# Turns of gates, latents, rotary keys, memory queries and conv operands by 32x32 VectorE blocks parked in DRAM, in a two-layer hybrid encoder

## The chip, the cores and the metric

The kernel runs on one core of one Trainium2 chip. Five engines matter here: TensorE (PE, with its weight loads shown apart as PEld), VectorE (DVE), ScalarE (ACT), GpSimd (POOL) and SyncE (SP). The metric is the time of one launch on the device in microseconds (us). Three runs of the kernel before took 1466.64, 1466.75 and 1467.07 us; the median is 1466.75 us.

## What is computed

Two layers of a sandwich-normalised mixer over 512 tokens of width 2048, all in fp32. Each layer projects the normalised input once into ten parts, feeds three groups of heads, gates their outputs and projects back:

```python
for l in range(DEPTH):                                     # DEPTH = 2
    h = rmsnorm(x, pre_norm_g[l])
    z = h @ w_in[l]                                        # 2048 x 4928
    q_lat, kv_lat, k_pe, gb, gc, xin, q_mem, gate = split_cols(z)
    q = (rmsnorm(q_lat, q_norm_g[l]) @ w_uq[l])            # 8 heads, rotary part turned
    kv = (rmsnorm(kv_lat, kv_norm_g[l]) @ w_ukv[l])
    a_out = mla_attention(q, k, v)                         # 8 heads, width 1024
    c_out = short_gated_conv(gb, gc, xin, conv_w[l])       # width 512
    m_out = memory_attention(q_mem, mem_n, ...)            # 4 heads, width 512
    mix = concatenate([a_out, c_out, m_out]) * silu(gate)
    x = x + rmsnorm(mix @ w_o[l], post_norm_g[l])
```

The convolution is `gb * conv3(gc * xin)`, three taps along the tokens for each channel. The latents, the rotary keys, the memory queries, the convolution and the gated mix are all needed with channels on the partitions, while the input projection leaves tokens on the partitions. So each of them has to be turned (transposed) once.

## The kernel before

**Arithmetic.** Each fp32 operand is split into a rounded part (hi) and the rest (lo), and a product is three matmuls, hi\*hi, hi\*lo and lo\*hi (`mm3`, L265 to L274). For the weights the split is made on the chip: ACT casts a piece of 128x1024 (`wh`, L189), then DVE subtracts (`wl`, L190). Each of `wh` and `wl` has three buffers; the raw pieces (`wr`) have eight, and are loaded by SP (L146), or added onto a piece that is there by a GpSimd DMA that accumulates (`more`, also L146). Where two pieces are added on the chip, DVE does so ahead of the cast (L178, the `sums` of a piece).

**The input projection** runs as five groups for each layer. A group computes a 2x2 block of column halves by seven products (a Strassen form) of combinations of the input (`P1` to `P7`). A plain group (`STEADY`) has 28 steps: four of P1, eight of P5 and P2 in turns, eight of P6 and P3 in turns, four of P7 and four of P4. Each step takes one weight piece through twelve matmuls 512 wide (416 wide in the latents' group). The order of the groups in `gs` before: 0 is gc and xi (convolution), 1 is gb and a gate, 2 is a gate `gm` with the memory queries `qm`, 3 is the latents with the rotary keys (`lat`), and 4 is the two gates `ga0` and `ga1`.

**The turns before.** gc\*xi and gb (`conv_turn`), the latents (`latent_turn`), the memory queries (`qm_turn`) are turned by PE, through `turn4` (L911 to L915): four matmuls with the identity fill one bank `tps` of 128x512, and ACT or DVE copy it out. The rotary keys go the same way (`k_rope_turn`, L1021, bank `krps`). The gates gm, ga0 and ga1 are turned already in 32x32 blocks by DVE (L933), and `exchange` (L941) then moves the blocks between partitions by sixteen DMAs from one SBUF tile to another.

**What sets the order.** Python code puts the steps one behind another. PE, SP and POOL keep that order. The instructions of DVE and ACT are put in order by a scheduler, engine by engine; at run time each engine takes its own list strictly in order. The preparation of a weight piece runs two steps ahead, its load up to eight. Small jobs that may come later are put off (`pr.defer`) and paid out beside the steps. The convolution's four chunks of 128 channels are woven into group 2, one in each second step.

The programs' names: `gc`, `gb`, `gm`, `qm`, `ga` are slabs of 128x2048, `y` is the gated mix, `P` is a PSUM bank of the projection, `ptp` a bank for turned attention probabilities, `sc` for scores, `u` and `cols` the convolution's input chunk and its taps.

## Time and profile before

The profiled execution took 1469.51 us; its span, from the first instruction to the last, is 1467.7 us.

| what | value |
|---|---|
| profiled execution / its span | 1469.51 us / 1467.7 us |
| PE busy | 1452.2 us in 7104 matmuls |
| PE weight loads | 1237.3 us |
| DVE busy | 1095.8 us in 1461 instructions |
| ACT busy | 869.6 us in 1328 instructions |
| POOL busy | 267.8 us |
| DMA | 295.22 MB, 201 GB/s on average |

A row of groups reads: line, engine, operation, output<-inputs, tile shape, number; then busy time in us and mean ns of one; then idle time ahead of them and what ended it. A matmul's duration is longer than the distance to the next one, since they are pipelined; a chain of waits shows the distance. A row of a timeline reads: start in us, duration in us, engine, line, operation, in square brackets the idle time ahead of it and what ended that. A row of the waits reads: who waited, for whom, us in total, times, longest.

### The profile page before, as it was taken

The numbers are of one execution on the slowest core, as the hardware profiler recorded it, in microseconds if no ns is written. First come the engines' busy times: TensorE is split into PE (matmuls) and PEld (weight loads), VectorE is DVE, ScalarE is ACT, GpSimd is POOL, SyncE is SP. The second block draws the span as 40 slices with busy tenths as digits, with TensorE's granted clock in tenths as the row PEclk, the third lists the DMA queues.
The fourth block names the chain that finished last, engine by engine and source line by source line (L and its number), as shares of the span: only waits on it lengthen the run. The fifth ranks groups of instructions, "written<-read, shape, count | busy, mean of one in ns | idle before, by whom it ended". The sixth has DMA issues, their size and how long they took to land.

```text
span 1467.7 us, 19472 instructions
## 1 busy us (share of the span) xinstructions
PE 1452.2 (99%) x7104; PEld 1237.3 (84%) x7104; DVE 1095.8 (75%) x1461; ACT 869.6 (59%) x1328; POOL 267.8 (18%) x272
## 2 busy tenths in 40 slices
PE   9999999999999999999999999999999999999997
PEld 7887888899888888888898888888998888888886
DVE  5899677857677778868789656766576776788687
ACT  7856445445458788654777434454464586786443
POOL 0032302031301010321220333030313001003111
PEclk9999999999999999999999999999999999999999
DMA  9999979797977292795987999696979674128983
GB/s 355 402 271 210 226 190 187 172 185 212 231 232 166 78 275 88 124 229 155 342 291 222 239 225 220 195 178 158 201 202 237 212 186 104 40 87 151 270 168 129
DMA packets 156672, 295.22 MB, mean 201 GB/s; under 512 B 11616, under 2 KB 46944, under 8 KB 152736
## 3 DMA queue, kind: packets, MB, share of 16 engines
q0 software_dynamic: 56000, 125.32, 42.7%
q1 hardware_dynamic: 100576, 168.65, 36.4%
q8 instruction: 56, 0.92, 0.3%
q14 instruction: 40, 0.33, 0.1%
HBM read 266.01 MB, written 21.63 MB: 196 GB/s over the span
## 4 chain that ended last, share of the span: by engine, by line
PE 84%; issue 5%; DMA 5%; POOL 3%; ACT 2%; DVE 1%; SPq 0%; POOLq 0%; DVEq 0%; ACTq 0%
PE P L273 20%; PE P L272 20%; PE P L274 20%; POOL wr L146 3%; DMA wr<-in_w_in_dram 3%; PE ptp L1198 2%; PE o L273 1%; PE o L274 1%; PE o L272 1%; PE sc L272 1%; PE sc L274 1%; PE sc L273 1%; PE tps L915 1%; PE sc L1179 1%; PE qps L272 1%
## 5 line engine op out<-in xcount | busy, mean ns | idle before, releaser
L190 DVE TENSOR_TENSOR wl<-wr,wh 128x1024 fp32r<-128x1024 f32 (+2 forms) x436 | 515.2, 1186 | 259.2 <-ACT wh L189 255.9
L189 ACT CAST wh<-wr 128x1024 fp32r<-128x1024 f32 (+2 forms) x436 | 443.9, 1023 | 444.5 <-PE P L274 329.4
L272 PE MATMUL P<-wh,S 128*128 128x512 f32 (+1 forms) x896 | 345.2, 385 | 0.0
L273 PE MATMUL P<-wl,S 128*128 128x512 f32 (+1 forms) x896 | 344.1, 384 | 0.8 <-DVE wl L190 0.8
L274 PE MATMUL P<-wh,S 128*128 128x512 f32 (+1 forms) x896 | 343.2, 383 | 0.0
L272 PE MATMUL P<-wh,A 128*128 128x512 f32 (+1 forms) x656 | 253.0, 386 | 0.0
L273 PE MATMUL P<-wl,A 128*128 128x512 f32 (+1 forms) x656 | 251.8, 384 | 1.2 <-DVE wl L190 1.2
L274 PE MATMUL P<-wh,A 128*128 128x512 f32 (+1 forms) x656 | 251.5, 383 | 0.0
L146 POOL DMA_DIRECT2D wr<-in_w_in_dram x132 | 158.9, 1204 | 446.1 <-DVE wl L190 272.6
L273 PEld LDWEIGHTS P<-wl,S 128*128 128x128 f32 x896 | 168.2, 188 | 31.2 <-DVE wl L190 1.8
L274 PEld LDWEIGHTS P<-wh,S 128*128 128x128 f32 x896 | 168.2, 188 | 30.2
L272 PEld LDWEIGHTS P<-wh,S 128*128 128x128 f32 x896 | 168.1, 188 | 29.9 <-ACT wh L189 0.2
L273 PEld LDWEIGHTS P<-wl,A 128*128 128x128 f32 x656 | 123.2, 188 | 23.4 <-DVE wl L190 2.0
L274 PEld LDWEIGHTS P<-wh,A 128*128 128x128 f32 x656 | 123.1, 188 | 22.3
L272 PEld LDWEIGHTS P<-wh,A 128*128 128x128 f32 x656 | 123.1, 188 | 21.8 <-ACT og L586 0.2
L146 POOL DMA_DIRECT2D wr<-in_w_o_dram x40 | 48.5, 1261 | 299.0 <-DVE wl L190 293.6
L1185 ACT ACTIVATE P<-sc,nm 128x512 f32<-128x512 f32 (+1 forms) x96 | 59.8, 623 | 28.6 <-DVE nm L1182 28.3
L1182 DVE TENSOR_REDUCE nm<-sc 128x1 f32<-128x512 f32 (+1 forms) x96 | 56.7, 594 | 14.3 <-PE sc L1180 9.0
L1188 ACT ACTIVATE P<-P,rec 128x512 f32<-128x512 f32 (+1 forms) x96 | 61.8, 660 | 8.0 <-DVE rec L1187 8.0
L1198 PE MATMUL ptp<-identr,P 128*128 128x128 f32 x320 | 46.2, 273 | 2.3 <-ACT P L1188 2.3
L1198 PEld LDWEIGHTS ptp<-identr,P 128*128 128x128 f32 x320 | 37.9, 140 | 8.9 <-ACT P L1188 3.0
L178 DVE TENSOR_TENSOR wr<-wr,wr 128x1024 f32<-128x1024 f32 (+1 forms) x36 | 42.2, 1174 | 2.6 <-DMA wr<-in_w_in_dram 2.1
(317 smaller groups left out, 2069.0 us busy)
## 6 DMA issues: line engine op xcount, KB each, us to landing
wr<-in_w_in_dram SPq DMA_DIRECT2D x128, 512.0 KB, 5.6
wr<-in_w_in_dram POOLq DMA_DIRECT2D x108, 512.0 KB, 7.5
wr<-in_w_o_dram SPq DMA_DIRECT2D x48, 512.0 KB, 6.3
wr<-in_w_o_dram POOLq DMA_DIRECT2D x40, 512.0 KB, 7.3
wr<-in_w_in_dram SPq DMA_DIRECT2D x32, 416.0 KB, 3.5
wr<-in_w_in_dram POOLq DMA_DIRECT2D x24, 416.0 KB, 6.0
wr<-in_w_mk_dram SPq DMA_DIRECT2D x15, 512.0 KB, 9.1
wr<-in_w_mv_dram SPq DMA_DIRECT2D x15, 512.0 KB, 10.5
```

The lines of the kernel that those rows point to most:

```text
L146: engine.dma_start(dst, src, **kw)
L178: nc.vector.tensor_tensor(tiles[a], tiles[a], tiles[b], op=ALU.add)
L189: pin(nc.scalar.copy(hi[:, h], src[:, h]))
L190: pin(nc.vector.tensor_tensor(lo[:, h], src[:, h], hi[:, h].bitcast(F32), op=ALU.subtract))
L272: nc.tensor.matmul(ps, ah, bh, start=first, stop=False, **kw)
L273: nc.tensor.matmul(ps, ah, bl, start=False, stop=False, **kw)
L274: nc.tensor.matmul(ps, al, bh, start=False, stop=last, **kw)
L915: nc.tensor.transpose(ps[:, t * P:(t + 1) * P], v[:, 4 * j:4 * j + 4].rearrange("p g j -> p (g j)") if len(v.shape) == 3 else v[:, j * P:( ...
L1182: nc.vector.tensor_reduce(nmax, ps, axis=AX.X, op=ALU.max, negate=True)
L1185: nc.scalar.activation(pt, ps, AF.Exp, bias=nmax, accum_out=tot)
L1188: nc.scalar.activation(pt, pt, AF.Copy, scale=rec)
L1198: nc.tensor.transpose(ps[:, k * P:(k + 1) * P], pt[:, k * P:(k + 1) * P], G["ident"])
```

## The change

The latents, the rotary keys, the memory queries and the convolution's two operands are no longer turned on PE. Each such slab, and each gate, is turned by DVE in 32x32 blocks (`STREAM_TRANSPOSE`), then one DMA parks it in DRAM (`sent`), and four DMAs fetch it back, a block row each (`fetched`). The columns of `w_in` and two norm gains are permuted on the host, so that the blocks fall where they are needed. What is fetched has its tokens in a permuted order; the matmuls read it through a view of four runs of 128 (`spots`). The convolution's chunks, the memory queries and the latents are computed from fetched slabs. The latents' group becomes the third of a layer and the group gm/qm the fourth. The weight block B22 of a `STEADY` group is loaded by SP once, with P6, and a sum on DVE adds it to T, where before SP loaded it for P3 and a GpSimd DMA accumulated it for P6. The left operand of the output projection is split in two halves in layer 0 too.

```diff
@@ Left.split
             if self.apart:
-                hi, lo = (t[:, o:o + 1024].rearrange("p (t g j) -> p g t j", t=2, j=32) for o in (0, 1024))
-                split_to(hi, lo, src.rearrange("p g (t j) -> p g t j", j=32))
+                if src.shape[-1] == P:
+                    split_to(t[:, :1024], t[:, 1024:], src.rearrange("q g k -> q (g k)"))
+                    return
...
+                for i in range(2):
+                    split_to(hi[:, i], lo[:, i], src[:, :, 32 * i:32 * i + 32].rearrange("q (p c) j -> q p c j", p=4))
@@ group
+            if passes is STEADY and q in ("P6", "P3"):
+                return of("T", [("B22", "B22")], sums=[("T", "B22")]) if q == "P6" else of("B22")
             return {"P5": ..., "P6": lambda: of("T", more="B22"),
@@ input projection
+        def turned(name, t):
+            def f():
+                nc.vector.transpose(C[name][:, t], C[name][:, t])
...
-            group(L, (l, 2), 512, block((O_G + 1536, O_QM), 512), slot_of("gm", "qm"), STEADY, fin_m),
-            group(L, (l, 3), 416, block((0, 416), 416), lat, STEADY, skip),
+            group(L, (l, 2), 416, block((0, 416), 416), lat, STEADY, skip),
+            group(L, (l, 3), 512, block((O_G + 1536, O_QM), 512), slot_of("gm", "qm"), STEADY, fin_m),
@@ turns
-    def turn4(view, j, dst=None):
...
-    def exchange(dst, src):
-        for p in range(4):
-            for b in range(4):
...
-                nc.sync.dma_start(dst[32 * b:32 * b + 32, :, P * p:P * p + P], a)
+    def spots(t, c=4):
+        return t.rearrange("q (p c k) -> q c p k", p=4, c=c)
+    def sent(key, *parts):
...
+            nc.sync.dma_start(d[:, :, o:o + w].rearrange("b q k -> q b k"), t.rearrange("q (b k) -> q b k", b=4))
+    def fetched(key, name, c=4):
+        t, d = slab(name), G.pop(("sent", key))
+        for b in range(4):
+            nc.sync.dma_start(t[32 * b:32 * b + 32, :512 * c].rearrange("i (p k) -> i p k", p=4),
+                              d[b].rearrange("(p i) k -> i p k", p=4))
+        return t
-    def conv_turn(l, c, C):
-            ps = turn4(lambda t: C["gc"][:, t], c)
...
+    def conv_back():
+        G["uw"] = fetched("gc", "u")
+        G["ys"][2] = spots(fetched("gb", "y"))
+    def conv(l, c):
+            u, y, w, g = scrap("u"), scrap("conv"), G[f"cw{l}"], G["ys"][2][:, c]
+            nc.scalar.copy(by_tokens(u), spots(G["uw"])[:, c])
             nc.scalar.activation(y, u, AF.Copy, scale=w[:, 1, c:c + 1])
...
+            nc.vector.tensor_tensor(g, by_tokens(y), g, op=ALU.mult)
@@ order of a layer
-        conv = [(conv_turn(l, c, C), []) for c in range(4)]
-        put(weave(gs[2][1] + gs[2][2], conv, 2), *gs[2][3:])
+        steps = [s for passes in gs[3] for s in passes]
+        put(steps[:2])
+        add(lambda l=l, C=C: latents_begin(l, C))
...
+        add(conv_back)
+        put(steps[8:12])
+        if l == 0:
+            add(tables_turned)
+        put(steps[12:14])
+        add(conv(l, 0))
+        put(steps[14:17])
+        add(lambda l=l: latents_sent(l))
+        put(steps[17:19])
+        add(conv(l, 1))
+        put(steps[19:22])
+        add(conv(l, 2))
+        put(steps[22:25])
+        add(conv(l, 3))
+        put(steps[25:])
...
-        G["left"] = Y = Left(False, l + 1 < depth)
+        G["left"] = Y = Left(False, True)
```

**PE, group gm/qm before, layer 0.** The rows stand in the second pass of the group, where the first convolution chunk is turned. `P` are the projection's banks, `S` is a left operand, `tps` the banks of the turns.

```order
L273 MATMUL P_92_1937<-wl_1893,A_29_624 128x512
L274 MATMUL P_92_1937<-wh_1892,A_29_624 128x512
L915 MATMUL tps_1950<-identr,gc_651 128x128 x4
L915 MATMUL tps_1961<-identr,gb_867 128x128 x4
L272 MATMUL P_89_1916<-wh_1911,S_59_1007 128x512
L273 MATMUL P_89_1916<-wl_1912,S_59_1007 128x512
L274 MATMUL P_89_1916<-wh_1911,S_59_1007 128x512
```

In the changed kernel these matmuls, and the other 152 of their kind, are gone, and nothing stands in their place on PE.

**DVE before, the same place.** `wl` is the lower part of a weight piece, L956, L957 and L960 are one chunk of the convolution.

```order
L190 TENSOR_TENSOR wl_1969<-wr_1714,wh_1968 128x1024
L956 SCALAR_TENSOR_TENSOR y_1955<-u_1956,cols,y_1955 128x511
L957 SCALAR_TENSOR_TENSOR y_1955<-u_1956,cols,y_1955 128x511
L960 TENSOR_TENSOR y_1955<-y_1955,tps_1961 128x4x4x32
L190 TENSOR_TENSOR wl_1988<-wr_1852,wh_1987 128x1024
L190 TENSOR_TENSOR wl_2021<-wr_1732,wh_2020 128x1024
L956 SCALAR_TENSOR_TENSOR y_1955<-u_2008,cols,y_1955 128x511
L957 SCALAR_TENSOR_TENSOR y_1955<-u_2008,cols,y_1955 128x511
L960 TENSOR_TENSOR y_1955<-y_1955,tps_2013 128x4x4x32
L190 TENSOR_TENSOR wl_2040<-wr_1890,wh_2039 128x1024
```

One chunk stands between each second pair of weight pieces.

**DVE after, group gm/qm (now the fourth), layer 0.** `wl_2761` belongs to the sixteenth step of the group (the second of P3), `wl_2788` to the seventeenth (the third of P6); L975, L976 and L978 are the three instructions of a chunk, L178 the sum of T and B22 for the pieces of P6.

```order
L190 TENSOR_TENSOR wl_2761<-wr_2582,wh_2760 128x1024
L975 SCALAR_TENSOR_TENSOR conv_2780<-u_2779,cols,conv_2780 128x511
L976 SCALAR_TENSOR_TENSOR conv_2780<-u_2779,cols,conv_2780 128x511
L975 SCALAR_TENSOR_TENSOR conv_2880<-u_2879,cols,conv_2880 128x511
L976 SCALAR_TENSOR_TENSOR conv_2880<-u_2879,cols,conv_2880 128x511
L975 SCALAR_TENSOR_TENSOR conv_2943<-u_2942,cols,conv_2943 128x511
L976 SCALAR_TENSOR_TENSOR conv_2943<-u_2942,cols,conv_2943 128x511
L978 TENSOR_TENSOR y_2639<-conv_2780,y_2639 128x4x128
L978 TENSOR_TENSOR y_2639<-conv_2880,y_2639 128x4x128
L978 TENSOR_TENSOR y_2639<-conv_2943,y_2639 128x4x128
L178 TENSOR_TENSOR wr_2311<-wr_2311,wr_2644 128x1024
L975 SCALAR_TENSOR_TENSOR conv_3010<-u_3009,cols,conv_3010 128x511
```

Straight behind them come the second sum and the pieces that follow.

```order
L178 TENSOR_TENSOR wr_2329<-wr_2329,wr_2680 128x1024
L190 TENSOR_TENSOR wl_2788<-wr_2311,wh_2787 128x1024
L190 TENSOR_TENSOR wl_2805<-wr_2644,wh_2804 128x1024
L190 TENSOR_TENSOR wl_2823<-wr_2329,wh_2822 128x1024
L976 SCALAR_TENSOR_TENSOR conv_3010<-u_3009,cols,conv_3010 128x511
L978 TENSOR_TENSOR y_2639<-conv_3010,y_2639 128x4x128
L190 TENSOR_TENSOR wl_2845<-wr_2680,wh_2844 128x1024
```

Three whole chunks and the first instruction of the fourth now stand between two neighbouring weight pieces, with two of the new sums. In layer 1 the same rows stand between the same two steps.

**ACT after, the same place.** `wh_2760` and `wh_2787` are the upper parts of the same two pieces; L973 and L974 are ACT's two instructions of a chunk.

```order
L189 CAST wh_2760<-wr_2582 128x1024
L973 COPY u_2779<-u_2634 128x512
L974 ACTIVATE conv_2780<-u_2779,cols 128x512
L973 COPY u_2879<-u_2634 128x512
L974 ACTIVATE conv_2880<-u_2879,cols 128x512
L973 COPY u_2942<-u_2634 128x512
L974 ACTIVATE conv_2943<-u_2942,cols 128x512
L973 COPY u_3009<-u_2634 128x512
L974 ACTIVATE conv_3010<-u_3009,cols 128x512
L189 CAST wh_2787<-wr_2311 128x1024
L189 CAST wh_2804<-wr_2644 128x1024
```

All four chunks stand ahead of `wh_2787`, which is cast from the piece `wr_2311` that the sum in the DVE rows writes.

More of the change, by code (lines that the diff above doesn't have):

```diff
@@ L907, in mem_fetch, with by_tokens @@
             G[n] = t.rearrange("p (s i c) -> p s i c", s=2, i=k)
-    def turn4(view, j, dst=None):
-        ps = bank("tps")
-        for t in range(NT):
-            v = view(t)
-            nc.tensor.transpose(ps[:, t * P:(t + 1) * P], v[:, 4 * j:4 * j + 4].rearrange("p g j -> p (g j)") if len(v.shape) == 3 else v[:, j * P:(j + 1) * P], G["ident"])
-        return ps
-    def y_slab(k):
-        if k not in G["ys"]:
-            G["ys"][k] = slab("y").rearrange("p (j c) -> p j c", j=4)
-        return G["ys"][k]
+    def spots(t, c=4):
+        return t.rearrange("q (p c k) -> q c p k", p=4, c=c)
+    def by_tokens(a):
+        return a.rearrange("q (p k) -> q p k", p=4)
     def of_tiles(a):
@@ L1470, in use @@
             G["ys"] = {}
+            for n in ("cq", "ckv", "Qm"):
+                G.pop(n, None)
         ms = mem_steps(l)
@@ L1589, in encoder @@
-        put(g4[2:8])
-        add(lambda C=C: k_rope(C))
-        put(g4[8:13])
-        add(gate_rows(3, "gm", C))
-        put(g4[13:16])
-        lat = [latent_turn(l, "cq", j) for j in range(4)] + [latent_turn(l, "ckv", j) for j in range(2)] + [k_rope_turn]
-        more = [(f, []) for f in lat + [qm_turn(j, C) for j in range(4)]]
-        put(weave(g4[16:], more, 2, 2)[:-2])
+        add(latents_back)
+        put(g4[2:6])
+        add(sent_rows("qm", C))
+        put(g4[6:8])
+        add(sent_rows("gm", C))
@@ L1597, in encoder @@
+        put(g4[8:9])
+        add(latents_parts)
+        put(g4[9:14])
+        add(lambda: G.update(qmw=fetched("qm", "QmL")))
+        put(g4[14:19])
+        add(qm_parts)
+        put(g4[19:22])
+        add(gate_back(3, "gm"))
+        put(g4[22:26])
         add(mem_fetch)
-        put(weave(g4[16:], more, 2, 2)[-2:])
-        G["left"] = Y = Left(False, l + 1 < depth)
+        put(g4[26:])
+        add(lambda: pr.until(lambda: "Qm" in G and "cq" in G))
+        G["left"] = Y = Left(False, True)
```

218 lines of the change are left out of this document (120 added, 98 removed).

## The prediction

> **What bounds the kernel now.** I read the page's busy times first, then the waits, then one step of the projection in the timeline.
>
> ```profile
> PE 1452.2 (99%) x7104; PEld 1237.3 (84%) x7104; DVE 1095.8 (75%) x1461; ACT 869.6 (59%) x1328; POOL 267.8 (18%) x272
> ...
> POOL wr L146 <- DVE wl L190: 566.2, 112, 82.7
> ACT wh L189 <- PE P L274: 332.5, 235, 2.2
> ...
> PE P L273 <- DVE wl L190: 1.9, 3, 0.8
> ...
> 448.11 0.44 PE L1198 MATMUL ptp<-identr,P 128*128 128x128 f32 x2 [1.13 <-ACT P L1188]
> ```
>
> TensorE is the bound: it stands idle for 1467.7 - 1452.2 = 15.5 us of the whole span. The waits say the same from the other side. ACT's casts wait 235 times for PE to let go of a weight buffer, while PE waits for a lower part on three occasions, 1.9 us in all. The longest gap in front of a PE matmul that I found is 1.13 us. So POOL's 566.2 us of waiting costs nothing, and only two things can move the end: work that leaves or joins PE, and a new stall of PE. Stalls that exist can give back at most 15.5 us.
>
> ```profile
> 388.69 1.05 ACT L189 CAST wh<-wr 128x1024 fp32r<-128x1024 f32 x1 [1.04 <-PE P L274]
> 391.41 1.05 ACT L189 CAST wh<-wr 128x1024 fp32r<-128x1024 f32 x1 [1.67 <-PE P L274]
> ...
> 387.54 1.18 DVE L190 TENSOR_TENSOR wl<-wr,wh 128x1024 fp32r<-128x1024 f32 x1
> 388.64 0.70 DVE L933 STREAM_TRANSPOSE ga<-ga 128x512 f32<-128x512 f32 x1
> ...
> 392.50 1.23 DVE L190 TENSOR_TENSOR wl<-wr,wh 128x1024 fp32r<-128x1024 f32 x1 [1.50 <-ACT wh L189]
> ```
>
> This is the rhythm of a 512-wide step: PE frees a buffer every 391.41 - 388.69 = 2.72 us, and the lower part that is made in it is ready at 392.50 + 1.23, which is 2.32 us after PE let go. With three buffers, a piece that starts when PE leaves step n is needed by step n+3. PE has then three steps to do, 3 x 2.72 = 8.16 us, so **the slack of a weight piece is 8.16 - 2.32 = 5.84 us**. Whatever holds DVE up for less is free.
>
> **What leaves PE.**
>
> ```profile
> L915 PE MATMUL tps<-identr,lat 128*128 128x128 f32 x48 | 6.2, 272 | 0.0
> L915 PE MATMUL tps<-identr,gb 128*128 128x128 f32 x32 | 4.8, 273 | 0.0
> L915 PE MATMUL tps<-identr,gc 128*128 128x128 f32 x32 | 4.8, 271 | 0.0
> ...
> L915 PE MATMUL tps<-identr,qm 128*128 128x128 f32 x32 | 4.5, 274 | 0.0
> ...
> 225.74 0.87 PE tps L915 x8
> ...
> 421.21 0.64 PE krps L1021 x8
> ```
>
> 144 turns through `tps` and 16 through `krps` go (48+32+32+32 of the first). Their mean of 272 ns isn't the price, since matmuls overlap; the chain of waits has the distance. Eight of the first took 0.87 us, so 144 take 144 x 0.109 = 15.7 us; eight of the second took 0.64, so 16 take 1.3 us. They stand on the path, since PE is never out of work beside them: **-17.0 us**. With no new stall that is the whole effect.
>
> **What joins PE.** No matmul is added, but many read their moving operand in four runs of 128 instead of one run of 512. The nearest rows:
>
> ```profile
> L272 PE MATMUL mk<-mH,wh 128*128 128x256 f32 x128 | 36.4, 284 | 0.0
> ...
> L272 PE MATMUL vps<-wh,ckv 128*128 128x256 f32 x64 | 18.1, 282 | 0.0
> ```
>
> The values' matmul (`vps`) reads its 256 columns in two runs of 128 with a gap between, the keys' matmul of the memory (`mk`) in one piece; 282 against 284 ns. I take 0, and bound it by those 2 ns each way, times some hundreds of matmuls: under 1 us.
>
> **What joins DVE, and what covers it.**
>
> ```profile
> L933 DVE STREAM_TRANSPOSE ga<-ga 128x512 f32<-128x512 f32 x16 | 11.1, 702 | 1.3 <-ACT ga L786 1.3
> ...
> L178 DVE TENSOR_TENSOR wr<-wr,wr 128x1024 f32<-128x1024 f32 (+1 forms) x36 | 42.2, 1174 | 2.6 <-DMA wr<-in_w_in_dram 2.1
> ...
> 220.00:240.00 20.00, 20.00 (x102) 16.84 (x101) 13.27 (x14) 10.76 (x13) 3.57 (x3) 1.00 0.94 209
> 280.00:300.00 20.00, 20.00 (x100) 18.35 (x99) 18.96 (x42) 10.96 (x16) 1.18 (x1) 1.00 0.53 139
> ```
>
> Turns: 24 more of 128x512 (gc, gb and qm, four tiles in each of two layers) at 0.702 us are 16.8 us. The latents' slabs, 3584 columns for each layer, are 7 such lengths, 4.9 us, twice 9.8. The sums of T and B22: three STEADY groups of four pieces in two layers, 24 at 1.17 us, 28.2 us. Together 55 us, and DVE goes from 1096 to about 1150 us, 78%. That by itself costs nothing: in the second stretch above (the columns are PE, PEld, DVE, ACT and POOL busy, then the clock, the DMA share and GB/s) DVE is busy for 18.96 of 20 us and PE still for all 20. It costs when it comes in a lump longer than 5.84 us between two weight pieces, because DVE takes its list in order.
>
> There is such a lump. In the fourth group three whole chunks of the convolution, two sums and a first instruction of the fourth chunk stand between the lower parts of the sixteenth and seventeenth step. Before, one chunk stood between two pieces:
>
> ```profile
> 226.73 0.58 ACT L954 COPY u<-tps 128x512 f32<-128x512 f32 x1
> 227.35 0.73 ACT L955 ACTIVATE y<-u,cols 128x512 f32<-128x512 f32 x1
> ...
> 226.86 1.23 DVE L190 TENSOR_TENSOR wl<-wr,wh 128x1024 fp32r<-128x1024 f32 x1 [1.49 <-ACT wh L189]
> 228.11 0.75 DVE L956 SCALAR_TENSOR_TENSOR y<-u,cols,y 128x511 f32<-128x511 f32 x1
> 228.89 0.75 DVE L957 SCALAR_TENSOR_TENSOR y<-u,cols,y 128x511 f32<-128x511 f32 x1
> 229.75 0.69 DVE L960 TENSOR_TENSOR y<-y,tps 128x512 f32<-128x512 f32 x1
> 230.47 1.23 DVE L190 TENSOR_TENSOR wl<-wr,wh 128x1024 fp32r<-128x1024 f32 x1
> ```
>
> From 228.11 to 230.47 a chunk takes 2.36 us. Counted from the moment at which PE frees the buffer of the sixteenth piece: 2.32 until its lower part, 3 x 2.36 = 7.08 for three chunks, 1.17 for the sum that writes the seventeenth piece, 0.75 for the stray instruction, 1.17 for the second sum, 1.23 for the lower part: 13.72 us. ACT isn't later: its cast of the seventeenth waits for the first sum (10.57) and ends 1.05 after, at 11.62, behind which the lower part waits only for DVE. PE has 8.16 us of steps, and one matmul of 0.23 us with the upper part, before it needs the lower. It stands still for 13.72 - 8.39 = **5.3 us, in each layer, 10.7 in all**.
>
> Bounds of that. From below: neighbours on DVE can overlap (387.54 + 1.18 is past 388.64 by 0.08), and the chunk's three durations are 2.19, not 2.36; thirteen overlaps and three times 0.17 take 1.5 off, 3.8 us for each layer. From above: a chunk takes two of the four small buffers (`piece`), so ACT may start the third chunk only when the first lets go, and such a wait for one pair of ACT's instructions, 0.58 + 0.73, adds 1.3, 6.6 us. So 7.6 to 13.2 for both layers; I take 10.7, from the row of a chunk itself. What hides nothing here: the copies on ACT stand ahead of the same cast, so ACT can't run ahead either.
>
> **Other edits.** The latents' group gets the turns of gb and gc, and its steps are shorter (416 of 512 columns, 2.72 x 0.81 = 2.21 us), so slack shrinks to about 4.3 us; in the last group the latents' parts are cut into halves of at most 1.2 us; in layer 0 the output projection's left operand is split in two. Each is one or two short instructions between two pieces, so I count 0.7 us for all, between 0 and 4. The 24 accumulating DMAs that leave POOL return nothing, as POOL's waits are off the path. B22 comes one step earlier:
>
> ```profile
> wr<-in_w_in_dram SPq DMA_DIRECT2D x128, 512.0 KB, 5.6
> wr<-in_w_in_dram POOLq DMA_DIRECT2D x108, 512.0 KB, 7.5
> ...
> y<-ga SPq DMA_DIRECT2D x64, 64.0 KB, 3.5
> ...
> 380.53 17.01 SPq L941 DMA_DIRECT2D y<-gm  x15
> ```
>
> It lands 5.6 us after its issue and is asked for six steps ahead, 16.3 us. On SP, fifteen issues of an exchange held the queue for 17.01 us, 1.13 each; the eight fetches for the convolution should hold it for 9.1, and 9.1 + 5.6 is still under 16.3. I take 0 for SP and bound it by the rival below.
>
> **The sum**, against the profiled execution's own 1469.5: -17.0 + 10.7 + 0.7 = -5.6, which gives 1463.9. That execution was 2.76 us above the median of the runs, 1466.75; on their scale the forecast is **1461.2 us**.
>
> [...] Row first: the granted clock is 1.00 in both stretches above, and with gaps of 1.13 us at most no row here shows PE after a long pause. [...]
>
> **Rivals.**
> - *The clock drops after the pause.* The stall has two parts: 11.62 - 8.16 = 3.5 us until the upper part, then one matmul, then 1.9 us. If the clock were halved for as long as that first pause, PE would lose 1.7 us more in each layer: 1461.2 + 3.5 = 1464.7 us. For it: the pause would be three times the longest of before. Against it: the clock of 1.00 in all that was read. [...] Chance 0.04.
> - *No lump.* If DVE reaches the chunks earlier, while PE has slack, or if its waits fall so that the sum comes first, the stall shrinks towards 0: 1469.5 - 17.0 - 2.8 = 1449.7 us without any, 1455 with half of it, and the case reaches up to 1457.5. Against it: DVE's list is strict. Chance 0.16.
> - *DVE's stretches stall PE elsewhere too*, in the latents' group or the output projection: 3 to 9 us more, 1464 to 1470. For it: DVE at 18.96 of 20 us has little left, and the slack in 416-wide steps is 4.3. Chance 0.17.
> - *Parked trips hold SP back (slower).* Each parked slab is one issue that waits for a turn and four that wait for the parking to land. If a fetch stands on SP until its send has landed (3.5 us, estimated from the row `y<-ga`), then 3.5 + 9.1 + 5.6 = 18.2 us against 16.3: the weight behind it is 1.9 us late. Sixteen trips in two layers would be 30 us, half of them 15: 1476 us. It decides from 0.53 us for each trip, (1469.7 - 1461.2) / 16. Against it: sends and fetches of the same slab stand many steps apart, and exchanges that held SP for 17.01 us left PE full. Chance 0.08.
>
> **How the numbers follow.** The forecast itself, 7.6 to 13.2 us of lump and 0 to 4 elsewhere, covers about 1457.5 to 1464 and has 0.55. About 0.2% is what a measurement of this kernel can tell from no change, so faster ends at 1463.8 and slower begins at 1469.7. Faster: nearly all of the forecast and the case without a lump, 0.68. Same: the rest of the forecast, the clock and nearly all of the stretches, 0.22. Slower: parked trips and the last of the stretches, 0.10. The range runs from 1450.0 to 1466.5: the forecast, the clock, nearly all of the case without a lump and half of the stretches.
>
> **What would show it.** Right: no `tps` or `krps` on PE, DVE near 1150 us, POOL's 108 issues of 512 KB at 92 (sixteen of the 24 that go have that size), and one PE gap of about 3.5 and 1.9 us in the fourth group of each layer, put down to `wh` or `wl`, with the convolution's rows in a line on DVE beside it. Wrong: no gap there (the lump was hidden), more gaps elsewhere, PE waiting for a weight's DMA behind a fetch, a granted clock under 1.00 behind the gap, or turns that took more or less than 0.109 us each off PE.

## The result and the profile after

The changed kernel takes 1504.51 us (median of 4 runs, 1499.51 to 1507.02), the kernel before 1466.70 (1465.78 to 1467.07): **2.55% slower**, ratio 1.0255, 95% interval 1.0224 to 1.0285. The forecast of 1461.2 us had the wrong sign, and the time lies outside its range. The profiled execution is the shortest of the four, 1499.51 us; it is 30.0 us longer than the profiled one of before.

First the page's busy times of the changed kernel, its row of the granted clock in 40 slices, its DMA queues and its chain of waits.

```profile
PE 1444.9 (96%) x6944; PEld 1225.9 (82%) x6944; DVE 1140.6 (76%) x1517; ACT 870.1 (58%) x1328; POOL 239.7 (16%) x248
...
PEclk9999999989999999999999999999999999999999
...
q1 hardware_dynamic: 105472, 194.86, 43.0%
q0 software_dynamic: 49472, 113.52, 36.5%
...
PE 63%; issue 16%; DMA 10%; DVE 5%; ACT 3%; POOL 2%; SPq 0%; POOLq 0%; DVEq 0%; ACTq 0%
```

PE lost its 160 turns (7104 - 6944), and yet its busy time fell by only 7.3 us, from 1452.2. Its idle time rose from 15.5 to 1497.7 - 1444.9 = 52.8 us. So the span is -7.3 + 37.3 = +30.0 us, and two questions remain: where 37.3 us of stalls come from, and why a busy time that should fall by 17.0 fell by 7.3. In the chain of waits PE holds 63% of the span, before 84%; DMA went from 5% to 10%.

The waits, as before: engine, line and what it waited for, then us in total, times, longest.

```profile
ACT wh L189 <- DMA wr<-in_w_in_dram: 60.3, 24, 8.1
...
PE P L272 <- ACT wh L189: 23.5, 5, 13.0
...
ACT u L973 <- DMA tabd<-tab: 9.1, 1, 9.1
...
PE P L273 <- DVE wl L190: 7.2, 9, 1.2
...
PE o L273 <- DVE PTl L278: 6.1, 2, 3.1
```

Before, PE's only entry of these three was 1.9 us. Now it stands 23.5 us for upper parts, on five occasions, of which one took 13.0. ACT itself waited up to 8.1 us for a weight's DMA (4.0 before), and once 9.1 us for the DMA that sends the tables (`tab`) to DRAM. All gaps of about 1 us and more in PE's timeline, each as [main part + what follows after one matmul or a few]:

| place | layer 0 | layer 1 |
|---|---|---|
| latents' group | 4.93 + 0.35 | 1.60 + 0.60 |
| group gm/qm, sixteenth to seventeenth step | 12.98 + 1.00 | 3.79 + 1.00 |
| fifth group | 1.22 | 1.20 + 0.99 |
| first attention product (`ptp`), 1.13 before | 2.00 | 2.00 |
| end of attention | 0.65 + 3.09 | 0.66 + 3.02 |

They sum to 41.1 of the 52.8 us. Of the 11.7 that are left, most lies at the program's two ends: PE's first matmul starts at 1.45 us, and its last one ends 8.3 us before the span does. Both are the same in the kernel before, where they make up 9.7 of the 15.5 us.

**The lump.** PE's timeline in group gm/qm, layer 0, then layer 1 (start, us, instruction, idle before and its releaser in brackets):

```profile
336.14 0.80 PE L272 MATMUL P<-wh,S 128*128 128x512 f32 x1 [12.98 <-ACT wh L189]
337.94 0.80 PE L273 MATMUL P<-wl,S 128*128 128x512 f32 x1 [1.00 <-DVE wl L190]
...
1069.79 0.80 PE L272 MATMUL P<-wh,S 128*128 128x512 f32 x1 [3.79 <-ACT wh L189]
1071.59 0.80 PE L273 MATMUL P<-wl,S 128*128 128x512 f32 x1 [1.00 <-DVE wl L190]
```

Layer 1 is the forecast case: 3.79 + 1.00 = 4.8 us where 5.3 was predicted, in the same two parts. DVE's timeline there shows the predicted row of chunk instructions and sums, one straight behind the other (a duration reaches a little past the next start):

```profile
1065.58 1.89 DVE L978 TENSOR_TENSOR y<-conv,y 128x512 f32<-128x512 f32 x3
1067.38 1.22 DVE L178 TENSOR_TENSOR wr<-wr,wr 128x1024 f32<-128x1024 f32 x1
1068.52 0.74 DVE L975 SCALAR_TENSOR_TENSOR conv<-u,cols,conv 128x511 f32<-128x511 f32 x1
1069.18 1.22 DVE L178 TENSOR_TENSOR wr<-wr,wr 128x1024 f32<-128x1024 f32 x1
1070.32 3.48 DVE L190 TENSOR_TENSOR wl<-wr,wh 128x1024 fp32r<-128x1024 f32 x3
```

Layer 0 is three times that. ACT's timeline tells why:

```profile
326.51 0.62 ACT L973 COPY u<-u 128x512 f32<-128x512 f32 x1 [9.10 <-DMA tabd<-tab]
...
335.04 2.94 ACT L189 CAST wh<-wr 128x1024 fp32r<-128x1024 f32 x3 [1.57 <-DVE wr L178]
```

A chunk's first copy needs a small buffer that a table (`tab`) still holds until its DMA to DRAM has read it. ACT stands for 9.10 us, with the weight cast of 335.04 behind it in its list, and PE behind that: 12.98 - 3.79 = 9.19 us more than in layer 1. The DMA issues of that stretch (305 to 337 us; size and median us to landing) show what was in flight beside the tables' DMA:

```profile
wr<-in_w_in_dram POOLq DMA_DIRECT2D x4, 512.0 KB, 12.9
...
sentql<-ql SPq DMA_DIRECT2D x1, 1024.0 KB, 18.8
sentkvl<-kvl SPq DMA_DIRECT2D x1, 512.0 KB, 24.3
tabd<-tab POOLq DMA_DIRECT2D x2, 256.0 KB, 13.0
```

Transfers take 9.6 to 24 us here. In the kernel before, the tables' DMA landed after 5.6 us, and an accumulated weight after 7.5 (medians of the whole kernel). Which transfers do it, the run conv_later shows below.

**The latents' group.** Its DMA issues at 230 to 265 us:

```profile
wr<-in_w_in_dram POOLq DMA_DIRECT2D x8, 416.0 KB, 9.2
...
sentgb<-gb SPq DMA_DIRECT2D x1, 1024.0 KB, 7.7
sentgc<-gc SPq DMA_DIRECT2D x1, 1024.0 KB, 14.2
```

And ACT's timeline behind them, the casts of the pieces that these DMAs complete:

```profile
263.41 2.46 ACT L189 CAST wh<-wr 128x832 fp32r<-128x832 f32 x3 [8.09 <-DMA wr<-in_w_in_dram]
```

gb and gc are parked, 1 MB each, just when the eight accumulating DMAs of this group run. Those land after 9.2 us; DMAs of that kind took 6.0 in the kernel before. The cast of an accumulated piece waits 8.09 us for its DMA, and PE stands for 4.93.

**The end of attention.** DVE's timeline in layer 0:

```profile
602.04 1.29 DVE L278 TENSOR_TENSOR PTl<-ptp,PTh 128x512 fp32r<-128x512 f32 x2 [0.85 <-PE sc L274]
603.25 1.28 DVE L278 TENSOR_TENSOR S<-y,S 128x512 fp32r<-128x512 f32 x2
604.45 1.28 DVE L278 TENSOR_TENSOR PTl<-ptp,PTh 128x512 fp32r<-128x512 f32 x2
```

The split of the output projection's left operand (`S`) slips between two lower parts of the attention weights (`PTl`), and PE waits 3.09 us for the second.

**The clock.** Windows of the changed kernel (length; busy PE, PEld, DVE, ACT, POOL; granted clock; DMA share; GB/s), first two stretches at half clock and then the one behind them:

```profile
262.72:269.55 6.83, 4.86 (x13) 4.25 (x14) 3.49 (x4) 2.96 (x4) 0.00 (x0) 0.50 0.48 155
327.60:341.25 13.65, 4.11 (x9) 2.92 (x10) 12.21 (x15) 5.96 (x8) 2.96 (x3) 0.50 0.54 111
341.30:345.00 3.70, 3.70 (x17) 3.05 (x17) 1.47 (x2) 1.06 (x2) 0.68 (x2) 1.00 1.11 192
```

PE's timeline behind the two long gaps at the end of attention, layer 0 and layer 1:

```profile
605.78 0.50 PE L273 MATMUL o<-PTl,V 128*128 128x512 f32 x1 [3.09 <-DVE PTl L278]
606.12 0.40 PE L274 MATMUL o<-PTh,V 128*128 128x512 f32 x1
...
1341.40 0.79 PE L273 MATMUL o<-PTl,V 128*128 128x512 f32 x1 [3.02 <-DVE PTl L278]
1342.00 0.63 PE L274 MATMUL o<-PTh,V 128*128 128x512 f32 x1
```

The trace's clock records hold four stretches at half clock before the program's last microseconds: 6.83 us (from 262.7), 13.65 (327.6), 6.83 (1068.3) and 3.41 (1341.3). The kernel before has none there. In the changed kernel's records these stretches start 64.85, 740.69 and 273.07 us apart, which is 19, 217 and 80 times 3.413 us. Three pieces of that length, counted on from the first start (columns as above), two for the pause of 3.09 us and one for that of 3.02:

```profile
600.63:604.04 3.41, 1.65 (x6) 1.05 (x6) 2.56 (x6) 3.14 (x8) 0.00 (x0) 1.00 0.53 153
604.04:607.45 3.41, 1.67 (x7) 1.41 (x8) 3.41 (x7) 2.18 (x5) 0.00 (x0) 1.00 0.00 0
1337.91:1341.32 3.41, 0.48 (x3) 0.04 (x1) 3.41 (x6) 2.42 (x3) 0.00 (x0) 1.00 0.12 44
```

The first pause is spread over two pieces, with PE idle for 1.76 and 1.74 us, and the clock behind them stays at 1.00; the second leaves PE idle for 2.93 us of one piece, and the 3.41 us behind it are at half clock.

A matmul of 512 columns, 0.39 to 0.40 us, takes 0.63 at half clock, and the distance to the next one is 0.43 instead of 0.23. 36 matmuls run so, which costs about 7 us. By the distances of the matmuls, the work at full clock fell by about 18 us, and the added gaps make matmuls at their edges longer by some 4. So the busy time: -18 + 7 + 4 = -7, as measured.

### The profile page after: what moved, and what is told of

It reads as the page before. It is cut to its first block, busy times and chain, and to the rows that moved or that the text cites. A ratio compares the mean times of both kernels' runs of the same rounds, so it can differ in the third digit from the quotient of the medians.

```text
span 1497.7 us, 19187 instructions
## 1 busy us (share of the span) xinstructions
PE 1444.9 (96%) x6944; PEld 1225.9 (82%) x6944; DVE 1140.6 (76%) x1517; ACT 870.1 (58%) x1328; POOL 239.7 (16%) x248
## 3 DMA queue, kind: packets, MB, share of 16 engines
q1 hardware_dynamic: 105472, 194.86, 43.0%
q0 software_dynamic: 49472, 113.52, 36.5%
## 4 chain that ended last, share of the span: by engine, by line
PE 63%; issue 16%; DMA 10%; DVE 5%; ACT 3%; POOL 2%; SPq 0%; POOLq 0%; DVEq 0%; ACTq 0%
PE P L273 14%; PE P L274 14%; PE P L272 14%; DMA wr<-in_w_in_dram 5%; POOL wr L146 2%; PE ptp L1217 2%; DVE wl L190 2%; DMA Km<-Kmd 1%; PE o L273 1%; ACT wh L189 1%; PE o L274 1%; PE o L272 1%; PE sc L272 1%; PE sc L273 1%; PE sc L274 1%
## 5 line engine op out<-in xcount | busy, mean ns | idle before, releaser
L272 PE MATMUL P<-wh,S 128*128 128x512 f32 (+1 forms) x896 | 346.9, 387 | 23.5 <-ACT wh L189 23.5
L146 POOL DMA_DIRECT2D wr<-in_w_in_dram x108 | 130.2, 1210 | 495.3 <-DVE wl L190 314.7
L178 DVE TENSOR_TENSOR wr<-wr,wr 128x1024 f32<-128x1024 f32 (+1 forms) x60 | 69.6, 1163 | 6.0 <-DMA wr<-in_w_in_dram 5.2
## 6 DMA issues: line engine op xcount, KB each, us to landing
wr<-in_w_mv_dram SPq DMA_DIRECT2D x15, 512.0 KB, 10.5
```

The costliest lines, as they stand in the source:

```text
L146: engine.dma_start(dst, src, **kw)
L178: nc.vector.tensor_tensor(tiles[a], tiles[a], tiles[b], op=ALU.add)
L272: nc.tensor.matmul(ps, ah, bh, start=first, stop=False, **kw)
```

## The experiments

After the first reading four accounts were open for the 38 us: a **lump** on DVE's and ACT's lists (as predicted), a **small buffer held** by the tables, **crowded DMA engines** (parked slabs delay the accumulating DMAs, so that the casts behind them are late), and the **clock**. Each run has the kernel before beside it (medians 1466.4 to 1466.7). Differences named below are between medians and, unless another kernel is named, against the changed kernel. Of the runs that change one thing, only b22_accum is clear of the changed kernel's interval; the others overlap it or touch it, so for those the places of the gaps in the traces carry the argument, not the time.

| run | median us | range | ratio, 95% interval |
|---|---|---|---|
| changed kernel | 1504.51 | 1499.51–1507.02 | 1.0255 [1.0224, 1.0285] |
| tab_late | 1497.01 | 1495.64–1498.86 | 1.0208 [1.0191, 1.0225] |
| code_order | 1499.92 | 1499.00–1501.09 | 1.0224 [1.0209, 1.0239] |
| sends_after | 1502.10 | 1500.21–1504.54 | 1.0239 [1.0224, 1.0255] |
| b22_accum | 1514.41 | 1513.03–1514.97 | 1.0321 [1.0306, 1.0336] |
| conv_later | 1498.55 | 1490.04–1502.33 | 1.0209 [1.0175, 1.0243] |
| sends_early | 1498.16 | 1493.74–1501.90 | 1.0213 [1.0190, 1.0236] |
| sums3 | 1496.34 | 1489.50–1499.84 | 1.0196 [1.0167, 1.0225] |
| all3 | 1478.26 | 1477.04–1479.76 | 1.0082 [1.0065, 1.0099] |
| conv_on_pe | 1470.38 | 1466.57–1474.33 | 1.0028 [1.0014, 1.0043] |
| warm_gap | 1503.90 | 1500.57–1506.92 | 1.0246 [1.0229, 1.0263] |
| b22_alone | 1472.17 | 1470.69–1474.04 | 1.0037 [1.0024, 1.0050] |
| conv_on_pe_accum | 1483.88 | 1480.95–1487.80 | 1.0113 [1.0096, 1.0130] |

### tab_late: the tables give their buffers back later

```diff
         put(steps[8:12])
-        if l == 0:
-            add(tables_turned)
...
         add(conv(l, 3))
         put(steps[25:])
+        if l == 0:
+            add(tables_turned)
```

> The two table turns of layer 0 are moved behind the convolution's chunks; nothing else of the code is moved. Theory 1 (order on ACT and DVE): in layer 0 ACT's copy for a chunk waits for a small buffer that the tables' DMA to DRAM still reads (9.1 us in the changed kernel), and the next weight cast stands behind it. Then the PE gap of 13.0 + 1.0 us in the fourth group of layer 0 falls to 5 us or less, the half clock behind it goes or shrinks, and the time falls by 9 to 13 us against the changed kernel's 1504.5, to about 1493. Layer 1 keeps its 3.8 + 1.0 us. Theory 2 (what is fetched from DRAM comes late): the gap stays at 13 us, since the fetches are as they were, and the time stays within 3 us.

Measured: -7.5 us, a little less than expected. The gap of 12.98 + 1.00 in layer 0 became 0.47 + 1.30, and ACT's wait for the tables' DMA is gone. This is less than the lump of layer 1, since in this run the scheduler also put the sums and weight pieces of layer 0 between the chunks: the run takes the held buffer and the lump away together. That the buffer is what tripled the gap rests on the trace of the changed kernel (9.10 us of waiting, 9.19 more than in layer 1) and on sends_after, sends_early and sums3: there ACT waits 8.5 to 9.7 us for `tabd`, and the gap is 12.4 to 13.9 us again. But a gap that wasn't there stands a little later in PE's timeline:

```profile
348.86 0.79 PE L272 MATMUL P<-wh,S 128*128 128x512 f32 x1 [3.48 <-ACT wh L189]
350.12 0.79 PE L273 MATMUL P<-wl,S 128*128 128x512 f32 x1 [0.47 <-DVE wl L190]
```

Here ACT waits 6.48 us for a weight's DMA. Some 12 us of stall went there, 4 came back. Layer 1 kept its lump (3.79 + 1.30).

### code_order: DVE and ACT in the order of the code

```diff
+        own_order = ExitStack()
+        add(lambda own_order=own_order: own_order.enter_context(tc.manual_schedule(
+            engines={mybir.EngineType.DVE, mybir.EngineType.Activation})))
         put(steps[12:14])
         add(conv(l, 0))
...
         put(steps[25:])
+        add(own_order.close)
```

> DVE and ACT keep the order of the code from the thirteenth step of the group gm/qm to its end, in both layers, so the convolution's chunks stand between weight pieces one by one; the tables stay where they are. Theory 1 (the lump in the lists of DVE and ACT): both gaps of the fourth group go (14.0 us in layer 0, 4.8 in layer 1) with the half clock behind them (about 5 us), and the time falls by 20 to 25 us against the changed kernel, to about 1481. Theory 2 (late data from the parked slabs or the tables' DMA): the first chunk waits just as long and the gaps stay, at 10 us or more in layer 0.

Measured: -4.6 us instead of 20 to 25. The lump is gone in both layers, by the windows of this run (columns as above); in the changed kernel the same two stretches had PE busy for 6.02 of 20 and 5.21 of 10 us:

```profile
322.00:342.00 20.00, 19.51 (x84) 15.22 (x82) 14.35 (x17) 7.37 (x8) 6.03 (x5) 1.00 1.10 256
1066.00:1076.00 10.00, 10.00 (x45) 8.04 (x44) 7.81 (x8) 5.32 (x7) 3.35 (x3) 1.00 1.10 248
```

The time isn't gained. Just behind, in PE's timeline of this run:

```profile
344.00 0.50 PE L272 MATMUL P<-wh,S 128*128 128x512 f32 x1 [2.00 <-ACT wh L189]
...
352.02 0.50 PE L272 MATMUL P<-wh,S 128*128 128x512 f32 x1 [2.38 <-ACT wh L189]
```

And in ACT's, the two casts that PE waits for there:

```profile
342.91 1.04 ACT L189 CAST wh<-wr 128x1024 fp32r<-128x1024 f32 x1 [5.05 <-DMA wr<-in_w_in_dram]
350.93 1.04 ACT L189 CAST wh<-wr 128x1024 fp32r<-128x1024 f32 x1 [6.98 <-DMA wr<-in_w_in_dram]
```

ACT now waits for weights: 90.9 us in the whole kernel, where the changed kernel has 60.3. A PE that doesn't pause asks for the accumulated pieces earlier, and they aren't there. The lump had been hiding late DMAs; **without it the landing of weights sets the pace behind it**. The DMA share of 1.10 doesn't show by itself that the engines are full: in the kernel before it is 1.03 from 305 to 337 us, and PE never stands still there.

One thing more: the tables stand where they stood, their DMA takes 13.8 us, and yet ACT never waits for it in this run. With weight pieces between the chunks, the held buffer cost nothing here.

### sends_after and sends_early: when gb and gc are parked

The first moves both sends behind the latents' group, the second moves them to its second and sixth step.

```diff
-        put(steps[6:12])
-        add(sent_rows(("gb", "gc")[l], C))
-        put(steps[12:15])
-        add(sent_rows(("gc", "gb")[l], C))
-        put(steps[15:])
+        put(steps[6:])
+        add(sent_rows(("gb", "gc")[l], C))
+        add(sent_rows(("gc", "gb")[l], C))
```

```diff
-        put(steps[:6])
...
+        put(steps[:2])
+        add(sent_rows(("gb", "gc")[l], C))
+        put(steps[2:6])
+        add(sent_rows(("gc", "gb")[l], C))
+        put(steps[6:])
```

> The two DMAs that park gb and gc are issued behind the last step of the latents' group instead of in its middle. Theory 1 (DMA crowding): in the changed kernel the parking (7.7 and 14.2 us to landing) lies beside the accumulating DMAs of P7 and P4, which land after 7.5 to 10.8 us instead of 5.3 to 6.6 before, and the cast of the last P7 piece waits 8.1 us for one. Then the gap of 4.9 + 0.4 us in the latents' group of layer 0 and that of 1.6 + 0.6 in layer 1 go, with 2.9 us of half clock, about 10 us less in all, 1494. Theory 2 (the table arithmetic on DVE holds the lower parts, which hold the accumulating DMAs): the gap of layer 0 stays at 4 us or more and that of layer 1 as well. The fourth group's gaps should stay or grow, as its fetches come closer behind the parking.

> gb and gc are parked at the second and sixth step of the latents' group instead of the twelfth and fifteenth, ahead of the accumulating DMAs. If the parking crowds those: they land in 5 to 7 us again, the gaps of the latents' group (4.9 + 0.4 in layer 0, 1.6 + 0.6 in layer 1) go with 2.9 us of half clock, and nothing new comes, since nothing is delayed here as it was with the later parking: 9 to 11 us off, about 1494. If it is DVE's table arithmetic: the gap of layer 0 stays.

Measured: -2.4 and -6.3 us, where 10 and 9 to 11 were expected. Both take the gap of the latents' group away (4.93 + 0.35 becomes 0.32 + 0.61 in layer 0). With the sends early, the accumulating DMAs at 230 to 265 us land as fast as before the change:

```profile
wr<-in_w_in_dram POOLq DMA_DIRECT2D x8, 416.0 KB, 5.6
```

The tables' arithmetic on DVE stands where it stood, so it was not the cause.

With the sends late, they collide with the next group instead: a gap of 3.57 us opens at 1034.25 and one of 1.66 at 284.6. So a parked slab costs what it is in flight beside.

### conv_later: the chunks in the attention stage

```diff
-        add(conv_back)
...
-        add(conv(l, 0))
...
+        between.setdefault(13, []).append((conv_back, []))
+        for c, k in enumerate((22, 25, 28, 31)):
+            between.setdefault(k, []).append((conv(l, c), []))
```

> The convolution's fetches from DRAM and its four chunks are moved out of the group gm/qm into the attention stage; all else is as changed. Theory 1 (the fourth group is hit twice: by the convolution's lump on DVE and ACT, and by its eight fetches, which crowd the accumulating DMAs of P7 and P4): both go, the gaps of 13.0 + 1.0 and 3.8 + 1.0 us vanish with 5 us of half clock, the accumulating DMAs of the group land in under 9 us instead of 12 to 16, and the time falls by about 24 us, to 1481. Theory 2 (the latents' parking alone crowds the group's DMAs): gaps of 2 to 5 us stay in front of P7's pieces, as in the kernel in code order, and the time stays above 1490.

Measured: -6.0 us instead of 24, in a wide range. In group gm/qm only 1.04 + 0.76 and 0.74 + 0.76 us are left. But the same chunks now stand between the small instructions of the attention, and there gaps of 0.4 to 1.9 us appear, some 10 us in both layers: PE's waits for `PTl` rise from 6.1 to 9.3 us. The attention has no more room on DVE and ACT than the projection.

This run also shows which transfers met in layer 0. From 300 to 330 us the latents are parked as before and the tables sent as before; only the convolution's eight fetches and its chunks are elsewhere:

```profile
sentql<-ql SPq DMA_DIRECT2D x1, 1024.0 KB, 6.3
tabd<-tab POOLq DMA_DIRECT2D x2, 256.0 KB, 6.3
```

In the changed kernel these took 18.8 and 13.0 us, and in code_order, which has the fetches but no lump, 18.8 and 13.8. So it is the fetches together with the parking that made the tables' DMA late, not the parking alone.

### sums3: the first split of the output projection three steps later

```diff
-        last_pair = {0: [(sums(0), []), g0[0][0]], 1: [g0[0][1]], 2: [g0[0][2]], 3: [g0[0][3]],
+        last_pair = {0: [g0[0][0]], 1: [g0[0][1]], 2: [g0[0][2]], 3: [(sums(0), []), g0[0][3]],
```

> The sums of the output projection's left operand are put off by three steps of the last pair of heads, so that their splits no longer stand between the two lower parts of the attention probabilities on DVE. The gaps of 0.65 + 3.1 us ahead of the first o matmuls in both layers go, with 1.7 us of half clock: 6 to 9 us off, about 1497. If the splits are not the cause, the gaps stay at 3 us.

Measured: -8.2 us by the medians, as expected from the gaps; the ranges overlap, and the profiled executions differ by 3.0 us only. The window of this run at the end of attention:

```profile
595.00:615.00 20.00, 20.00 (x102) 16.73 (x101) 16.82 (x27) 15.27 (x28) 0.00 (x0) 1.00 0.26 80
```

The same window of the changed kernel:

```profile
595.00:615.00 20.00, 16.26 (x79) 12.86 (x78) 11.82 (x21) 12.22 (x22) 0.35 (x1) 1.00 0.17 51
```

Nothing takes the place of this gap here, so the split is shown to be its cause. The DMA share is 0.17 to 0.26: it is the one stall without much traffic around it. Whether its whole length came back, the time can't say: in the profiled execution PE's gaps shrank by 5.4 us, and the stretches at half clock grew (mean clock 0.987 against 0.988).

### all3: conv_later, sends_early and sums3 together

> The three edits together. If the parts are independent, 1504.5 - 24 - 10 - 8 = 1462, below the kernel before. If what is taken away in one stage comes back as crowding in the next, less than three quarters of the sum comes, and the time stays above 1472.

Measured: -26.3 us. By the medians that is more than the three alone (6.0 + 6.3 + 8.2 = 20.5), but their ranges are too wide to call the difference shown; against the forecast, it is less than three quarters of 42. The time is 12 us above the kernel before. The mean clock is back from 0.988 to 0.996. What is left lies mostly in the attention, as these two lines of PE's timeline show:

```profile
473.92 0.50 PE L272 MATMUL kps<-ckvH,wh 128*128 128x512 f32 x1 [0.80 <-ACT P L1204]
...
488.92 0.39 PE L272 MATMUL vps<-wh,ckvH 128*128 128x256 f32 x1 [1.38 <-DVE K L278]
```

### conv_on_pe and conv_on_pe_accum: gb and gc turned on PE again

gb and gc are neither parked nor fetched; their 64 turns go back to PE, spread over the latents' group as before over gm/qm. The tables come one group earlier, and sums3 is included. The second run also accumulates B22 by GpSimd's DMA again.

```diff
-BLOCKS = "gc", "gb", "gm", "qm", "ga0", "ga1"
+BLOCKS = "gm", "qm", "ga0", "ga1"
...
-        add(conv_back)
...
+        conv = [(conv_turn(l, c, C), []) for c in range(4)]
+        put(steps[:2], weave(steps[2:], conv, 4))
```

> Only the latents, the rotary keys, the memory queries and the gates are turned by DVE blocks and parked; gc and gb are turned on PE again, 64 matmuls, 7.0 us, and the convolution's chunks are woven into the latents' group, one for each four steps; the tables' arithmetic is moved one group ahead; the output projection's sums are put off as in the kernel sums3. Theory 1 (the stalls come from the parked conv operands, by DMA crowding and by the lump): the gaps of the latents' group and of the fourth group are gone, PE is 10.4 us shorter than before, and what is left of stalls (the last group's 1.2, the ptp gap 0.9 longer, in both layers) takes 4 to 6 us back: 1460 to 1463, faster than before. Theory 2 (any parked trip beside accumulating DMAs stalls PE): gaps of 3 us or more stay in the fourth or fifth group, and the time stays above 1470.

> The kernel conv_on_pe with B22 loaded for P3 and accumulated for P6 by GpSimd again. Theory 1 (the sums on DVE cost some 5.7 us wherever they stand, as they did alone in the kernel before): 1464 to 1466, a little faster than before. Theory 2 (24 accumulating DMAs beside what is still parked are late, as in the changed kernel, where they cost 10 us): 1475 to 1480.

Measured: 1470.38 us, 34 us less than the changed kernel and 0.28% [0.14, 0.43] more than the kernel before. PE still has 96 turns less, 10.5 us by the prediction's 0.109, and doesn't earn them: one gap of 1.48 + 0.76 us is left in group gm/qm, the two of 2.00 at the first attention product, and three of 0.9 to 1.2 elsewhere. The gaps of the latents' group and the lumps are gone, as the first theory says, but the forecast of 1460 to 1463 was missed by 7 us. With the accumulations the time is 13.5 us longer, 4 us beyond the second theory of that run. The accumulations show in PE's waits, by the waits of conv_on_pe_accum:

```profile
PE P L273 <- DVE wl L190: 9.3, 12, 1.9
PE P L272 <- ACT wh L189: 7.2, 4, 3.4
```

In conv_on_pe these were 7.1 and 1.7 us. The rest is clock: by the distances of the matmuls, half clock costs 8.7 us with the accumulations and 1.4 without (mean clock 0.991 and 0.997).

### b22_accum and b22_alone: the change of B22 by itself

The first undoes that edit in the changed kernel, the second makes it alone in the kernel before.

```diff
-            if passes is STEADY and q in ("P6", "P3"):
-                return of("T", [("B22", "B22")], sums=[("T", "B22")]) if q == "P6" else of("B22")
```

```diff
+            if passes is STEADY and q in ("P6", "P3"):
+                return of("T", [("B22", "B22")], sums=[("T", "B22")]) if q == "P6" else of("B22")
```

> B22 is loaded for P3 and accumulated for P6 by GpSimd again, as before the change; the rest is as changed. Theory 1 (DMA crowding is what makes weights late, and an accumulating DMA is dear for it): 24 accumulating DMAs come back, twelve of them beside parked slabs, so the gap in the latents' group of layer 0 grows from 5.3 to 8 us or more; against that the lump of layer 1 loses two sums, 2.3 us, and shrinks from 4.8 to about 2.5. The time is 0 to 10 us longer than the changed kernel's. Theory 2 (DVE is what runs out): 24 sums fewer, 28 us of DVE, make gaps shorter everywhere, and the time falls by 5 us or more.

> The kernel before with one edit of the change alone: B22 is loaded once and summed on DVE. Theory 1 (before, DMAs had room to spare where they are needed, and DVE as well): PE's work and its gaps stay, and the time is within 0.2% of 1466.7. Theory 2 (24 sums on DVE stall PE by themselves): gaps in the STEADY groups and 3 us or more on top.

Measured: +9.9 us against the changed kernel, and +5.8 us against the kernel before. The same edit costs 5.8 us in the kernel before and saves 10 to 13.5 in the changed one and in conv_on_pe. So the accumulating DMAs became dear through the rest of the change: with them, ACT's waits for weights are 81.8 us against 60.3 in the changed kernel. The way is not the expected one. The gap in the latents' group of layer 0 did not grow (4.50 + 0.60), and PE's gaps sum to the same as in the changed kernel (43.3 and 43.1 us behind the first matmul). But they are shorter and more of them, and eleven stretches at half clock stand where there were four: 108 matmuls run so instead of 36, about 20 us lost instead of 7, with a mean clock of 0.983 against 0.988. Where the 5.8 us go in the kernel before isn't settled. The profiled execution of b22_alone, 1470.69 us, has a PE idle for 1468.9 - 1452.4 = 16.5 us, against 15.5; and the profiled execution of before, with which one must compare it, was itself 2.8 us above its median.

### warm_gap: PE kept busy in the gap

```diff
-        put(steps[14:17])
+        put(steps[14:16])
+        if l == 0:
+            add(lambda: warm(52))
+        put(steps[16:17])
```

> As changed, with 52 matmuls (11.8 us) on PE in layer 0 ahead of the seventeenth step of the group gm/qm, where PE waits for 13 us; nothing reads their output. Theory 1 (the clock is lowered by the pause): the matmuls cost nothing, the half clock of 13.7 us there is gone, and the time falls by 2 to 3 us, which the medians may not tell but the clock of the stretch does. Theory 2 (the clock is lowered for another reason, or the work delays the preparation): the half clock stays, or the time grows by up to 11.8 us.

Measured: 1503.90 us, no change. The half clock in that place shrank from 13.65 to 3.41 us (from 322 to 342 us the mean clock is 0.91, in the changed kernel 0.66), so here it came with the pause. Yet from the last matmul of the sixteenth step to 200 matmuls of the program later it took 61.5 us, in the changed kernel 61.7. The run doesn't price the clock, since it saved almost none of the half clock that matters: most of the 13.65 us lay in the pause itself, where PE had nothing to do, and behind the pause 9 matmuls ran at half clock. Here pauses of 1.08 and 1.31 us are left, the clock is at half again beside them, and 7 matmuls ran so.

## Why the prediction was wrong

Point by point, in the order of its steps:

- **What leaves PE, -17.0: right.** The `tps` and `krps` rows are gone, 160 turns, and by the distances of the matmuls the work at full clock fell by about 18 us.
- **What joins PE, 0 within 1 us: not contradicted.** The 18 us leave no room for a dearer operand in four runs.
- **What joins DVE, about 1150 us: right in size** (1140.6; POOL's issues of 512 KB fell to 92 as predicted), and the lump stands between the two named steps, in the two named parts. In layer 1 it measured 4.8 us instead of 5.3.
- **The lump in layer 0: the step that failed is its upper bound.** "ACT may start the third chunk only when the first lets go ... adds 1.3": I counted the chunks as the only users of the small buffers. The tables take the same pool, and give a buffer back when a DMA lands, which took 13.0 us. The lump was 14.0 us, 8.7 above its forecast; the trace shows ACT's wait, and in tab_late both go. The bounds were also added up wrongly: with 13.2 of lump and 4 elsewhere the sum ends at 1466.9 us, not at 1464.
- **"Other edits", 0.7 us, 0 to 4: the largest error.** Latents' group 7.5, end of attention 7.4, fifth group 3.4 and first attention product 4.0 - 2.3 make about 20 us. Two mechanisms make 15 of them, each shown by its own run: parked slabs beside accumulating DMAs (sends_early) and the split of `S` between two `PTl` (sums3). The other 5, in the fifth group and at the first attention product, no run explains; the two at the attention product stay at 2.0 us or more in every version of the changed kernel. I had weighed each as "one or two short instructions" for DVE, and the first isn't an instruction of DVE at all.
- **"I take 0 for SP": the wrong resource.** The bound was a queue that is held. SP's queue wasn't: the eight fetches of layer 0 issued in 4.6 us (300.94 to 305.51), not in the 9.1 I allowed, and its longest hold there, 4.6 us for one issue of the latents' parking (311.11 to 315.68), was over 20 us before the gap ended. What was late was the landing. Whether the DMA engines, the order in the queues or DRAM was short isn't told apart by these runs. The change adds 194.86 - 168.65 = 26 MB on the plain queue and takes 12 MB from the other. The landing times that I took, such as 5.6 us, were medians of a kernel in which no slab of 1 MB was in flight beside the weights.
- **"The accumulating DMAs that leave POOL return nothing, as POOL's waits are off the path": failed in both directions.** The edit costs 5.8 us alone and is worth 10 to 13.5 with the parking. POOL's own waits were no measure of it. ACT's waits for landed weights aren't one by their sum either: 53.0 us before, 60.3 changed, 81.8 in b22_accum, but 90.9 in code_order, which is no slower than the changed kernel. What counts is which of them outlast the slack of a weight piece, and whether PE then loses its clock.
- **The clock, chance 0.04: it fell in both layers.** It cost about 7 us; the rival had 3.5. It had them from a half clock as long as the first pause, a length that was my assumption and that no run shows: in the fourth group the first pauses were 12.98 and 3.79 us, and half clock went on for 5.1 and 5.3 us from the first matmul behind them. Half clock also followed pauses of 2.00 and 2.38 us in code_order (mean clock 0.83 from 342 to 362 us), but not one of 3.09 in the changed kernel (605.78). Its idle time is spread over the two pieces shown above; whether that is why, no run tells. I judged from a trace in which PE, from its first matmul to its last, never paused for more than 1.13 us, and so couldn't tell what a longer pause does.
- **The rivals.** "Stretches stall PE elsewhere too" came true, at about 20 us instead of 3 to 9; "parked trips" named the right objects and the wrong place, SP's queue.

From -5.6 to +30.0 us in the profiled executions, the forecast missed by 35.6. Of these, the "other edits" make 19.3, the lump 18.8 - 10.7 = 8.1, and the half clock with the longer matmuls at the gaps about 11; the small rest takes some 3 off. That the lump of layer 1 came out as worked out was no luck: its place, its two parts and its rows are those of the forecast.

Removing one stall at a time returned 2 to 8 us, three at once 26. Part of a freed stall came back as other waits, about two thirds in code_order (18.8 us freed, the sum of the gaps only 6.1 shorter), until the traffic of gb and gc itself went (conv_on_pe). What stays open: the 5.8 us of b22_alone, and why conv_on_pe, with 96 turns less on PE, is still 4 us behind the kernel before; its small stalls were found, not their causes. No version here is faster than the kernel before.

## What to carry to other kernels

When a kernel's bound engine is 99% busy, an operation taken off it pays only as far as its replacement opens no new wait. Price a replacement that goes through DRAM by how long every transfer beside it then takes to land, above all the slowest kind with the least slack, and not by the queue that issues it. For each buffer that a moved instruction takes, list every user of that pool and when it lets go; where one lets go by a DMA, the wait is a landing time. And remove suspected stalls together as well as one by one, since a stall can hide the next one.

## What the runs showed of the hardware

- The granted clock stood at 1.00 or at 0.50 in the stretches of the changed kernel shown above. Its stretches at half clock behind pauses last 3.41, 6.83 and 13.65 us, and start 19, 217 and 80 times 3.413 us apart. With this trace cut into pieces of that length and PE's idle time taken as in the windows, no piece at full clock with up to 1.76 us of idle PE (600.63) was followed by half clock, and each with 2.14 us (1488.10) or more was. Pauses of nearly the same length went both ways (3.09 us: stayed, 3.02 us: halved).
- The software queue (q0), which carries the accumulating DMAs, took more engine time for a byte than the plain one (q1): in the changed kernel 36.5% for 113.52 MB against 43.0% for 194.86 MB, 1.46 times as much; in the kernel before, 42.7% for 125.32 MB against 36.4% for 168.65 MB, 1.58 times.
- An accumulating DMA of 416 KB landed after 5.6 (sends_early) to 6.0 us (the kernel before) without parked slabs beside it, after 9.2 with two of 1 MB (changed kernel, 230 to 265 us); those of 512 KB after 12.9 (changed kernel, 305 to 337 us) beside the latents' slabs and the convolution's fetches, where the slabs took 18.8 to 24.3 us themselves, and after 8.4 in conv_later, where the fetches were elsewhere and the slabs took 6.3 to 7.3.
